# A hybrid encoder on one core: eighteen of the down projection's inner tiles by seven products

## The chip, the core and the metric

One core of one Trainium2 chip. The metric is the device time of one execution in microseconds; the time before is the median of three runs. One of the executions was profiled, and all rows of the trace are from that one.

Engines: PE is TensorE (matmuls, with its weight loads as PEld), DVE is VectorE, ACT is ScalarE, POOL is GpSimd, SP is SyncE, which here only issues DMAs. Each engine does its instructions in the order in which the built program has them.

## The reference

One layer of an encoder over 1024 tokens with 1024 channels, all in float32. The change touches the last part alone, the gated feed-forward and what follows it:

```python
h2 = _rmsnorm(x, ffn_norm_w)
up = h2 @ w_up                                  # 1024 x 5632: gate and value, 2816 columns each
gate = _dwconv_centred(gate, dw_w, dw_b)        # three taps along the tokens
x = x + (silu(gate) * val) @ w_down             # 2816 x 1024
return _rmsnorm(x, final_norm_w)
```

Before it come a projection into the mixers, a convolution module, a chunkwise recurrence in two directions, and the output projection.

## The kernel before

Activations lie with channels on the 128 partitions and tokens along the free dimension, in two halves of 512. So the feed-forward's inner width 2816 is 22 inner tiles of 128 channels (`NF` = 22), and the outer width 8 tiles (`ND` = 8).

Every float32 product is made of three matmuls in a reduced format. An operand is cast to its high part on ACT (`A.copy`, profile L122) and the rest, source minus high part, is made on DVE (L119); together this is `split`. `mm3` (L144 to L146) then adds high x high, high x low and low x high into one PSUM bank. A weight column of `nk` tiles is split at once, in one page of `nk` x 128 columns.

The up projection takes two output tiles as one job, the gate's and the value's of one inner tile j (`ffn_job(j)`, by way of `pair_job`). With the inner sum cut in two (`nk` = 4 tiles each), the outputs in two tiles and the tokens in two halves, this is a 2 x 2 by 2 x 2 block product, and it is made with seven products instead of eight, numbered 1, 2, 6, 7, 5, 4, 3 in the order in which PE does them. Products 1, 6, 5 and 3 go into one bank (`row`, tag mm), each on top of the one before, products 7 and 4 into a second (`col`, tag sc), product 2 into a third (tag tr). After each product the bank is copied or added out before the next one that adds into it; ACT's copies into `su` are L270, the additions on DVE are `evac`, L1278 to L1285.

The weight sides of the seven products are sums of the four weight blocks, and the DMA queues make them. `rows` (tag wr, two buffers) and `col` (tag sw, one buffer) are loaded by SP; POOL then issues DMAs that add into a page on the way (L242): sw <- src1, then wr <- sw into one half of `rows`, then wr <- wr into the other half. `rows` is split twice: as loaded for products 1 and 2, and after both adds for products 6 and 3. `col` is split for products 7 and 5, and a fourth page, w4, for product 4. Weight pages with the splits: four of tag wp, three of tag wq.

`run_jobs` runs a list of such jobs. A job's `run` yields after every two inner tiles (a piece), and the next job's `prep` is called four pieces into the job; `Stream.fill(n)` advances by n pieces. PE's order is the order of the code. For the other engines a scheduler sets the order of the built program, so a cast that stands late in the code can run early.

The feed-forward's gating (in `evac`, L1284 to L1304) runs when the last product of a job has come out: scale by the norm (rstd2), then for each half ACT's first tap (L1289), two taps on DVE (L1293), SiLU on ACT (L1301), two multiplications on DVE (L1302, L1303), and the store of the half to `d_g` in DRAM (L1304).

In its first job the feed-forward waits for the sums of squares: `rstd_over_partitions` (L416 spreads them, L417 copies the result), in the code after seven pieces of job 0. The operands for products 4 and 3 (`hy`) are loaded and split after that (`late_parts`, `late_load`, with an adding DMA, L1334).

The down projection takes inner tiles in groups of 4, 4, 5, 5 and 4. `load_g` brings the tiles of a group from `d_g` and splits them; `std_job` multiplies for each of 8 output tiles and both halves, and `add_evac` (L1369) adds to the result `xr` in SBUF. Its count of matmuls is 22 x 8 x 2 x 3 = 1056. In the last group the residual is added, the tile is turned to tokens on the partitions (`turn_out`, L1410), the sums of squares are taken, and `finish` scales and stores.

Of the kernel before, what the change touches and what calls it, by code (L numbers as in the profile page):

```python
# [10 lines left out]
F32 = mybir.dt.float32  # L11
# [17 lines left out]
BASE_STEPS = 2  # L29
H = 512  # L30
# [15 lines left out]
def tile_hybrid_encoder(  # L46
# [71 lines left out]
    def split_lo(eng, lo, src, hi):  # L118
        eng.tensor_tensor(lo, src, hi.bitcast(F32), op=ALU.subtract)  # L119

    def split(hi, lo, src, eng):
        A.copy(hi, src)  # L122
        split_lo(eng, lo, src, hi)
        return hi, lo
# [22 lines left out]

    def run_jobs(jobs, lead=0, prime=0):  # L150


# [3 lines left out]
        def prepare(n):  # L156
            while jobs and len(ready) < n:
                prep, run = jobs.popleft()
                ready.append((run, prep()))

# [3 lines left out]
        while ready:  # L164
            run, w = ready.popleft()
            pieces = run(w)
            for _ in itertools.islice(pieces, lead):
                yield
            prepare(1)
            yield from pieces  # L170
            prepare(1)
# [53 lines left out]
    def pair_job(src0, src1, nk, acts, wpool, pool, evac, su=4, first=False):  # L225
# [7 lines left out]
        def prep():  # L233
            def both(src, alt):
                hi, lo = split(w_page(2 * nk, alt), w_page(2 * nk, alt), src, V)
                return [(hi[:, :nk], lo[:, :nk]), (hi[:, nk:], lo[:, nk:])]
# [7 lines left out]
            w = {}  # L244
# [6 lines left out]
            add(col, raw_w(src1, 2 * nk) if first else src1)  # L251
            w[1], w[2] = both(rows, None)
            add(rows[:, :nk], col[:, nk:])
            w[7], w[5] = both(col, pool)
            add(rows[:, nk:], rows[:, :nk])
            w[6], w[3] = both(rows, None)
            one = w_page(2 * nk, pool)
            w[4] = split(one[:, :nk], one[:, nk:], a22, V)
            return w

        def run(w):
# [6 lines left out]
            def copy(acc):  # L268
                t = page(pool, "su", su)
                A.copy(t, acc)  # L270
                return t

            row, b2, col = bank("mm"), bank("tr"), bank("sc")
            yield from product(1, row)
            p1 = copy(row)
            yield from product(2, b2)
            evac(0, 0, b2, p1, ALU.add)
            yield from product(6, row, False)
            u2 = copy(row)
            yield from product(7, col)  # L280
            p7 = copy(col)
            yield from product(5, row, False)
            evac(1, 1, p7, row, ALU.subtract)
            yield from product(4, col, False)
            evac(1, 0, col, u2, ALU.subtract)
            yield from product(3, row, False)
            evac(0, 1, row)
# [109 lines left out]
    d_g = scratch("d_g", NF, 2)  # L397

# [836 lines left out]
    h2_pages[7] = [[page(fw, "h7", 2 * NK2, F32R) for _ in range(2)] for _ in range(NK2)]  # L1235
# [27 lines left out]

    fu = tc.alloc_tile_pool(name="fu", bufs=1, reuse_waits="tile")

# [4 lines left out]

    def ffn_job(j):
        g = gp[j % 2]
        val = [None, None]

        def evac(e, half, x0, x1=None, op=None):
            if e == 1:
                val[half] = page(fu, "ft", 4)
# [6 lines left out]
            V.tensor_tensor(g[:, 1 : 1 + H], g[:, 1 : 1 + H], rstd2[0], op=ALU.mult)  # L1284
            V.tensor_tensor(gh, x0, rstd2[1], op=ALU.mult)  # L1285
            for hf in range(2):
                o = hf * H
                c = tmp()
                A.activation(  # L1289
                    c, g[:, o : o + H], AF.Identity, scale=vec("fdw", j), bias=vec("fdb", j)  # L1290
                )
                for k in (1, 2):
                    V.scalar_tensor_tensor(  # L1293
                        c,
                        g[:, o + k : o + k + H],
                        vec("fdw", k * NF + j),
                        c,
                        op0=ALU.mult,
                        op1=ALU.add,
                    )  # L1300
                A.activation(c, c, AF.Silu)  # L1301
                V.tensor_tensor(c, c, rstd2[hf], op=ALU.mult)  # L1302
                V.tensor_tensor(val[hf], val[hf], c, op=ALU.mult)  # L1303
                nc.sync.dma_start(d_g[j][hf], val[hf])  # L1304
# [7 lines left out]
            fu,  # L1312
            evac,
        )

    s_ffn = Stream(run_jobs([ffn_job(j) for j in range(NF)], 4))
# [4 lines left out]
    s_ffn.fill(5)  # L1321
    rstd2 = [next(st) for st in stats]

    def late_parts(i, src):
        h2[i].append(split(page(fu, "hy", 16, F32R), page(fu, "hy", 16, F32R), src, V))

    def late_load(src):
        t = page(fu, "ft", 4)
        nc.sync.dma_start(t, src)
        return t  # L1330

    for k in range(NK2):
        b21 = late_load(d_t6[k])
        G.dma_start(b21, d_h2[k + NK2][0], accum_op=ALU.add)  # L1334
        late_parts(4, b21)
    for k in range(NK2):
        late_parts(3, late_load(d_h2[k + NK2][1]))
    s_ffn.drain()
    fu.release()
    fw.release()  # L1340
# [3 lines left out]

    n_g = itertools.cycle([0] * 32 + [1] * 16)

    def g_page():
        return hx() if next(n_g) == 0 else page(fd, "gx", 16, F32R)

    groups = [4, 4, 5, 5, 4]  # L1350
    gs, jobs = [], []

# [140 lines left out]
```

## Time and profile before

| | us |
|---|---|
| median of three runs | 1862.43 (1860.35 to 1862.73) |
| the profiled execution | 1861.67 |
| its span in the trace | 1859.9 |

| stage, us from the span's start | what |
|---|---|
| up to 1150 | all before the feed-forward |
| 1150 to 1593 | the up projection, 22 jobs |
| 1593 to 1793 | down projection, four groups (18 inner tiles) |
| from 1793 | last group (4 inner tiles), final norm, output |

How to read the rows: the page gives busy time, share of the span and the number of instructions of each engine. A row of the stages gives the stretch, its length, busy time and count for each engine, the granted TensorE clock (1.00 is full), the mean busy share of the 16 DMA engines, and GB/s. A row of the waits gives who waited for which line, us in total, how often, and the longest. A row of the timeline gives start, duration, engine, line, operation and tiles, and in brackets how long the engine was idle before it and what ended that. A row of the chain gives start, duration and what. Successive matmuls overlap: their starts lie closer together than their durations.

### The profile page before, as it was taken

How to read it: one execution, taken by the hardware profiler on the slowest of the kernel's cores; microseconds unless marked ns; L12 is line 12 of the kernel's file. 1: busy time of each engine (PE TensorE's matmuls, PEld its weight loads, DVE VectorE, ACT ScalarE, POOL GpSimd, SP SyncE). 2: the span in 40 equal slices, each digit the busy share in tenths (PEclk: the TensorE clock that was granted, in tenths of full speed). 3: DMA queues.
4: the chain of work that ended last, by engine and by line, in shares of the span. 5: the costliest groups of instructions: out<-in, count | busy, mean ns of one | idle time of the engine just before them, and what ended most of it. 6: DMA issues, size and time to landing. Idle time of an engine off the chain costs nothing.

```text
span 1859.9 us, 23747 instructions
## 1 busy us (share of the span) xinstructions
PE 1778.8 (96%) x8574; PEld 1475.4 (79%) x8574; DVE 1275.2 (69%) x1878; ACT 793.9 (43%) x1482; POOL 172.9 (9%) x189
## 2 busy tenths in 40 slices
PE   8989999999999999999989999899999999999996
PEld 6877877887778888888878787677888888788885
DVE  4599999645479999999835565566666767534445
ACT  6443333334555556555442144443343434522124
POOL 1201111111000000000000001211111111000000
PEclk9999999999999999999999999999999999999998
DMA  7657878874753333332238566876676765733135
GB/s 271 215 146 181 180 175 197 198 173 135 222 170 95 109 114 114 110 105 93 73 120 231 182 210 197 177 163 137 149 155 150 151 155 124 218 95 95 56 87 170
DMA packets 324620, 283.51 MB, mean 152 GB/s; under 512 B 14862, under 2 KB 247062, under 8 KB 324502
## 3 DMA queue, kind: packets, MB, share of 16 engines
q1 hardware_dynamic: 273462, 241.10, 41.5%
q0 software_dynamic: 51040, 40.90, 15.2%
q8 instruction: 67, 1.10, 0.2%
q14 instruction: 51, 0.42, 0.1%
HBM read 189.14 MB, written 72.88 MB: 141 GB/s over the span
## 4 chain that ended last, share of the span: by engine, by line
PE 56%; DVE 20%; DMA 13%; ACT 5%; issue 4%; POOL 1%; SPq 0%; DVEq 0%; ACTq 0%; POOLq 0%
PE mm L144 14%; PE mm L145 14%; PE mm L146 13%; DMA tm<-d_a 3%; PE sc L144 3%; PE sc L146 3%; PE sc L145 3%; DVE wp L119 2%; DVE acc L756 2%; DMA wr<-wr 2%; DVE kG L841 2%; DVE DE L841 2%; DVE qF L841 1%; DMA sw<-in_w_in_dram 1%; DMA wr<-sw 1%
## 5 line engine op out<-in xcount | busy, mean ns | idle before, releaser
L144 PE MATMUL mm<-hx,wp 128*128 128x512 f32 x1176 | 477.4, 406 | 19.4 <-DVE ev L541 7.8
L146 PE MATMUL mm<-hx,wp 128*128 128x512 f32 x1176 | 462.5, 393 | 2.9 <-DVE wp L119 2.9
L145 PE MATMUL mm<-hx,wp 128*128 128x512 f32 x1176 | 462.4, 393 | 1.7 <-DVE hx L476 1.7
L122 ACT CAST wp<-wr 128x1024 fp32r<-128x1024 f32 (+2 forms) x193 | 176.6, 915 | 330.2 <-PE mm L145 191.7
L119 DVE TENSOR_TENSOR wp<-wr,wp 128x1024 fp32r<-128x1024 f32 (+2 forms) x193 | 203.5, 1055 | 111.6 <-ACT wp L122 102.0
L144 PEld LDWEIGHTS mm<-hx,wp 128*128 128x128 f32 x1176 | 223.1, 190 | 66.9 <-DVE ev L541 10.3
L146 PEld LDWEIGHTS mm<-hx,wp 128*128 128x128 f32 x1176 | 222.7, 189 | 53.1 <-DVE wp L119 4.6
L145 PEld LDWEIGHTS mm<-hx,wp 128*128 128x128 f32 x1176 | 223.2, 190 | 43.6 <-DVE hx L476 2.0
L756 DVE SCALAR_TENSOR_TENSOR acc<-gl,v_b,acc 128x1024 f32<-128x1024 f32 x120 | 149.4, 1280 | 0.4
L1369 DVE TENSOR_TENSOR xr<-mm,xr 128x512 f32<-128x512 f32 x48 | 33.2, 691 | 80.6 <-PE mm L146 80.6
L949 PE MATMUL sc<-qF,A 128*128 128x128 f32 x512 | 69.2, 279 | 14.0 <-DVE qF L841 13.2
L949 PEld LDWEIGHTS sc<-qF,A 128*128 128x128 f32 x512 | 64.6, 193 | 20.9 <-issue 16.8
L242 POOL DMA_DIRECT2D wr<-sw x38 | 33.7, 887 | 439.8 <-DVE wp L119 176.0
L122 ACT CAST wq<-sw 128x1024 fp32r<-128x1024 f32 x39 | 41.0, 1051 | 75.0 <-PE mm L145 61.0
L946 ACT COPY A<-kG 128x512 f32<-128x512 f32 x64 | 39.6, 618 | 73.5 <-DVE kG L841 51.0
L1293 DVE SCALAR_TENSOR_TENSOR tm<-gp,v_a,tm 128x512 f32<-128x512 f32 x88 | 65.8, 748 | 2.5 <-ACT tm L1289 1.7
L144 PE MATMUL mm<-hy,wp 128*128 128x512 f32 x156 | 61.2, 393 | 1.9 <-ACT su L270 1.9
L144 PE MATMUL tr<-hx,wp 128*128 128x512 f32 x156 | 61.3, 393 | 0.0
L145 PE MATMUL mm<-hy,wp 128*128 128x512 f32 x156 | 61.2, 392 | 0.0
L144 PE MATMUL sc<-hy,wq 128*128 128x512 f32 x156 | 61.1, 392 | 0.0
L146 PE MATMUL sc<-hy,wq 128*128 128x512 f32 x156 | 61.0, 391 | 0.0
L145 PE MATMUL sc<-hy,wq 128*128 128x512 f32 x156 | 60.8, 390 | 0.0
(322 smaller groups left out, 3573.1 us busy)
## 6 DMA issues: line engine op xcount, KB each, us to landing
wr<-in_w_in_dram SPq DMA_DIRECT2D x53, 512.0 KB, 4.9
sw<-in_ffn_w_up_dram SPq DMA_DIRECT2D x44, 256.0 KB, 4.7
sw<-in_ffn_w_up_dram POOLq DMA_DIRECT2D x22, 512.0 KB, 8.7
wr<-in_ffn_w_up_dram SPq DMA_DIRECT2D x22, 512.0 KB, 7.0
d_g<-ft SPq DMA_DIRECT2D x44, 256.0 KB, 3.8
ev<-d_g SPq DMA_DIRECT2D x44, 256.0 KB, 3.4
wr<-sw POOLq DMA_DIRECT2D x38, 256.0 KB, 3.2
wr<-wr POOLq DMA_DIRECT2D x38, 256.0 KB, 4.8
```

Source lines behind the costliest of these rows:

```text
L119: eng.tensor_tensor(lo, src, hi.bitcast(F32), op=ALU.subtract)
L122: A.copy(hi, src)
L144: T.matmul(acc, whi[:, k, :], ahi, start=first, stop=False, skip_group_check=again)
L145: T.matmul(acc, whi[:, k, :], alo, start=False, stop=False, skip_group_check=again)
L146: T.matmul(acc, wlo[:, k, :], ahi, start=False, stop=last, skip_group_check=again)
L242: G.dma_start(o, a, accum_op=ALU.add)
L756: V.scalar_tensor_tensor(acc, g[:, k : k + S], tap(k), acc, op0=ALU.mult, op1=ALU.add)
L841: V.tensor_tensor(o, a, b, op=op)
L946: A.copy(A_t.rearrange("p (b x e) -> p b x e", x=2, e=h), pairs(kG, h))
L949: T.matmul(b[:, c * P : (c + 1) * P].rearrange("p (b x e) -> p b x e", x=2, e=h), A_t[:, c * P : (c + 1) * P], view(qF, c * P, [[2 * h, P ...
L1293: V.scalar_tensor_tensor(c, g[:, o + k : o + k + H], vec("fdw", k * NF + j), c, op0=ALU.mult, op1=ALU.add,)
L1369: V.tensor_tensor(xr[i][half], acc, xr[i][half], op=ALU.add)
```

## The change

It has three parts.

1. The first 18 inner tiles of the down projection, as three groups of six, go by seven products too: `down_seven(n, m)` takes two output tiles and six inner tiles (`nk` = 3) as one job of `pair_job`, 12 jobs in all, in the same stream as the feed-forward's jobs. The seven activation sides are three of the four blocks themselves and four sums of them. `down_operands` makes the sums on DVE in the feed-forward and SP stores them in `d_t`: jobs at places 3, 4 and 5 of each six load their partner's tiles back (`mate`, from `d_g[j - 3]`), so that it is called nine times, each time at the end of `gated(1)`, which runs in the job after. The seven products are added straight to `xr` (`taps`). The last four inner tiles go by `std_job` as before, half by half.
2. Casts and gating are spread over pieces. `pair_job`'s `prep` becomes a generator of steps (`Weights`): loads at once, the split for products 1 and 2 three pieces later, that for 7 and 5 four later, for 6 and 3 three later, for 4 three later. `gated(hf)` is put off by 3 and 5 pieces with `later`. The operands of the down projection come in by a list of events: a load four pieces ahead of its split. The parts for products 4 and 3 of the feed-forward's operands are put off in the same way.
3. `pin` (`tc.keep_in_program_order`) keeps the scheduler from moving these casts, their subtractions and the two activations of the gating (all but the last job's) from their place in the code.

```diff
+    pin = tc.keep_in_program_order
+
+    def split(hi, lo, src, eng, late=False):
+        parts = A.copy(hi, src), eng.tensor_tensor(lo, src, hi.bitcast(F32), op=ALU.subtract)
+        if late:
+            for i in parts:
+                pin(i)
         return hi, lo
...
+    class Weights:
+        def __init__(self, steps):
+            self.parts = {}
+            self.steps, self.wait = steps(self.parts), 0
+            self.tick()
+
+        def tick(self):
+            self.wait -= 1
+            if self.wait <= 0:
+                self.wait = next(self.steps, 1 << 30)
+
+        def __getitem__(self, i):
+            while i not in self.parts:
+                self.wait = 0
+                self.tick()
+            return self.parts[i]
...
             for _ in itertools.islice(pieces, lead):
+                tick()
                 yield
             prepare(1)
...
+            yield 3
             w[1], w[2] = both(rows, None)
             add(rows[:, :nk], col[:, nk:])
+            add(rows[:, nk:], rows[:, :nk])
+            yield 4
             w[7], w[5] = both(col, pool)
-            add(rows[:, nk:], rows[:, :nk])
+            yield 3
             w[6], w[3] = both(rows, None)
+            yield 3
             one = w_page(2 * nk, pool)
-            w[4] = split(one[:, :nk], one[:, nk:], a22, V)
-            return w
+            w[4] = split(one[:, :nk], one[:, nk:], a22, V, late)
...
+    def down_operands(k, b11, b12, b21, b22):
+
+        t7, t6 = ft(), ft()
+        V.tensor_tensor(t7, b12, b22, op=ALU.subtract)
+        V.tensor_tensor(t6, t7, b11, op=ALU.subtract)
+        V.tensor_tensor(b12, b11, b12, op=ALU.subtract)
+        V.tensor_tensor(b11, b21, t6, op=ALU.add)
+        for i, t in ((7, t7), (6, t6), (5, b12), (4, b11)):
+            nc.sync.dma_start(d_t[i - 4][k], t)
...
+        def gated(hf):
...
+            V.tensor_tensor(val[hf], val[hf], c, op=ALU.mult)
+            nc.sync.dma_start(d_g[j][hf], val[hf])
+            if hf == 1 and mate:
+                down_operands(3 * group + place - 3, *mate, *val)
...
             for hf in range(2):
...
+                later(3 + 2 * hf, lambda hf=hf: gated(hf))
+            if group < NSEVEN and place >= 3:
+                for hf in range(2):
+                    mate.append(ft())
+                    nc.sync.dma_start(mate[hf], d_g[j - 3][hf])
...
+    def down_seven(n, m):
+        def taps(i, acc):
...
+            t = xr[2 * m + e][half]
+            if n > 0:
+                V.tensor_tensor(t, t, acc, op=op)
+            elif i in (1, 6, 7, 3):
+                A.copy(t, acc)
...
+        return pair_job(
+            cols(2 * m), cols(2 * m + 1), 3, lambda i: ops[n][i], fw, fv, None, late=True, taps=taps
+        )
...
+    def come_in(at, dst, src):
...
+        events.append((at - 4, 0, load_it))
+        events.append((at, 1, parts))
+
+    for n in range(NSEVEN):
+        loads = [operand(n, i, k) for i in PRODUCTS for k in range(3)]
+        if n == 0:
+            at = [PAIR * (NF - 1) + 3 + x + x // 9 for x in range(21)]
+        else:
+            at = [PAIR * (NF + 4 * n - 4) + 16 + 4 * x for x in range(5)]
+            at += [PAIR * (NF + 4 * n - 1) + 3 + int(1.2 * x) for x in range(16)]
...
-    groups = [4, 4, 5, 5, 4]
...
+    for half in range(2):
+        st = Stream(run_jobs(down_jobs(f0, NF - f0, (half,), final_evac)))
```

`PAIR` is 14, the pieces of a job; `NSEVEN` is 3, the groups of six. In the last feed-forward job product 3 is done ahead of product 4, in a bank of its own (`apart`). The output is stored in halves of its width, from pages of 512 columns.

308 lines of the change are left out of this document (191 added, 117 removed).

## The prediction

> **What bounds the kernel now.** I read the page first, then the busy time by stage, then PE's waits from the feed-forward on, then one steady feed-forward job on all engines.
>
> ```profile
> span 1859.9 us, 23747 instructions
> PE 1778.8 (96%) x8574; PEld 1475.4 (79%) x8574; DVE 1275.2 (69%) x1878; ACT 793.9 (43%) x1482; POOL 172.9 (9%) x189
> ```
> ```profile
> core 0: us, PE busy (x) PEld busy (x) DVE busy (x) ACT busy (x) POOL busy (x), PEclk, DMA share, GB/s
> 1314.00:1545.00 231.00, 231.00 (x1007) 188.93 (x1006) 154.18 (x204) 95.04 (x132) 39.75 (x37) 1.00 0.71 152
> 1700.00:1798.00 98.00, 98.00 (x434) 81.22 (x433) 35.93 (x52) 13.09 (x19) 0.00 (x0) 1.00 0.18 51
> ```
> ```profile
> PE sc L416 <- ACT rs L417: 6.1, 1, 6.1
> PE mm L144 <- ACT su L270: 4.9, 4, 1.6
> PE mm L144 <- ACT xr L1363: 3.2, 1, 3.2
> ```
>
> PE is the bound: no idle time in steady feed-forward and down projection. One matmul costs 231/1007 = 0.229 us in the feed-forward and 98/434 = 0.226 us in the down projection. What PE waits for is small: 6.1 us where the feed-forward starts, 4.9 us for copies of early products, 3.2 us at the seam to the down projection. The DMA engines are 71% busy in the feed-forward and 18% in the down projection: what makes weights for seven products is dear in transfers.
>
> The steady feed-forward job, rows of the timeline by engine:
>
> ```profile
> 1399.57 0.69 DVE L1285 TENSOR_TENSOR gp<-mm,rs 128x512 f32<-128x512 f32 x1 [1.35 <-PE mm L146]
> ...
> 1402.83 1.23 DVE L119 TENSOR_TENSOR wp<-wr,wp 128x1024 fp32r<-128x1024 f32 x1 [1.79 <-ACT wp L122]
> 1404.07 0.69 DVE L1302 TENSOR_TENSOR tm<-tm,rs 128x512 f32<-128x512 f32 x1
> ...
> 1409.20 1.22 DVE L119 TENSOR_TENSOR wp<-wr,wp 128x1024 fp32r<-128x1024 f32 x1
> ...
> 1418.85 0.69 DVE L1285 TENSOR_TENSOR gp<-mm,rs 128x512 f32<-128x512 f32 x1 [1.36 <-PE mm L146]
> ```
> ```profile
> 1401.75 1.05 ACT L122 CAST wp<-wr 128x1024 fp32r<-128x1024 f32 x1 [4.26 <-DMA wr<-wr]
> ...
> 1406.72 0.63 ACT L1301 ACTIVATE tm<-tm 128x512 f32<-128x512 f32 x1 [2.22 <-DVE tm L1293]
> ...
> 1420.16 1.05 ACT L122 CAST wp<-wr 128x1024 fp32r<-128x1024 f32 x1 [3.40 <-DMA wr<-wr]
> ```
> ```profile
> 1396.42 0.84 POOL L242 DMA_DIRECT2D wr<-wr  x1 [2.66 <-DMA wr<-sw]
> 1402.63 1.57 POOL L242 DMA_DIRECT2D sw<-in_ffn_w_up_dram  x1 [5.37 <-DMA sw<-in_ffn_w_up_dram]
> 1411.79 0.87 POOL L242 DMA_DIRECT2D wr<-sw  x1 [7.58 <-DMA d_g<-ft]
> 1415.30 0.85 POOL L242 DMA_DIRECT2D wr<-wr  x1 [2.64 <-DMA wr<-sw]
> 1421.43 1.56 POOL L242 DMA_DIRECT2D sw<-in_ffn_w_up_dram  x1 [5.28 <-DMA sw<-in_ffn_w_up_dram]
> ```
> ```profile
> 1415.48 0.38 SPq L247 DMA_DIRECT2D sw<-in_ffn_w_up_dram  x1
> ```
>
> A job lasts 1418.85 - 1399.57 = 19.28 us (84 matmuls at 0.229). Call the subtraction at 1402.83 s63 (low parts of products 6 and 3, this job) and the one at 1409.20 s12 (products 1 and 2, next job). They are tied in a ring: s63 -> later work in DVE's order -> s12 -> POOL adds into the same rows (wr<-sw, then wr<-wr) -> cast and s63 of the next job, without which PE cannot do product 6, the third of seven. That POOL waits for s12 a row of an earlier job shows:
>
> ```profile
> 1140.74 1.23 DVE L119 TENSOR_TENSOR wp<-wr,wp 128x1024 fp32r<-128x1024 f32 x1 [0.17 <-ACT wp L122]
> ```
> ```profile
> 1142.26 0.88 POOL L242 DMA_DIRECT2D wr<-sw  x1 [146.77 <-DVE wp L119]
> ```
>
> The ring now: s63 end to s12 end 1410.42 - 1404.06 = 6.4; start of POOL 1142.26 - 1141.97 = 0.3; wr<-sw 1415.30 - 1411.79 = 3.5; wr<-wr 1420.16 - 1415.30 = 4.9; cast to s63 end 1404.06 - 1401.75 = 2.3. Sum 17.4 us, 1.9 below the job, so PE never sees it.
>
> **The change, part by part.**
>
> *Matmuls.* The built program has 108 fewer: 864 become 756. Before 864 x 0.226 = 195.1 us; after, at the feed-forward's pitch (weights come the same way), 756 x 0.229 = 173.4: -21.7 us, if nothing else waits.
>
> *Plain feed-forward jobs.* gated() is now called 3 and 5 pieces into the next job, and the casts are held in program order. In the built order DVE now runs, between s63 and s12: the split of operand 4, four L1293, two L1302, two L1303, two evacuations; all of the gating work, part of which ran ahead of s63 before. That is 11 operations; eight took 1409.20 - 1404.07 = 5.13 us, 0.64 each, so 7.0. The second SiLU (0.63, ACT) has nothing on DVE beside it: +0.75 with two hand-overs. Directly dependent neighbours and the first SiLU's rest: +0.4, an estimate. s12 itself 1.2. So 9.4 in place of 6.4, and the ring is 9.4 + 0.3 + 3.5 + 4.9 + 2.3 = 20.4 us: longer than 19.3. PE waits 1.1 us at product 6 of each such job. There are 11: +12 us.
>
> *Jobs with down_operands* (9, places 4, 5, 0 of each six). Four more subtractions or additions and one evacuation stand ahead of s12: 5 x 0.64 = 3.2. Ring 23.6, +4.3 a job. In the third of each three the built order puts s63 behind three other operations, so only 13 remain between: 8.3 + 0.75 + 1.2 = 10.3, ring 21.3, +2.0. Sum 6 x 4.3 + 3 x 2.0 = +32. Their six extra transfers (2 loads, 4 stores of 256 KB) are SP's, ahead of the next sw load; that load's own chain has slack while the ring waits.
>
> Of the 4.9 us of L270 waits, in four pauses, one (1.6) stands at the start; the other 3.3 are replaced. Feed-forward: 12 + 32 - 3.3 = +41. Bounds: if both adds take 3.5 us, plain jobs lose nothing and the nine lose 2.9, 2.9, 0.6: +16 after the same deduction. If wr<-wr takes 1401.75 - 1396.42 = 5.3, and the extra transfers (1.57 MB beside 2.9 MB a job, on engines 71% busy) add 3 us in the nine: 11 x 1.5 + 6 x 7.7 + 3 x 5.4 - 3.3 = +75. I take the steady row.
>
> A rule of the Trainium skill speaks for the lower bound. "DMA: Bandwidth & Descriptors", section "Anatomy of one DMA", puts a transfer issued by GpSimd at about 2.0 us fixed plus bytes/436e3: 2.6 us for 256 KB, one add like the other. By it the ring would be 9.4 + 0.3 + 5.2 + 2.3 = 17.2 and plain jobs would lose nothing. The trace disagrees: 3.5 and 4.9.
>
> *The feed-forward's start.*
>
> ```profile
> 1150.33 0.39 PE L146 MATMUL mm<-mg,wp 128*128 128x512 f32 x1
> 1150.56 0.39 PE L144 MATMUL mm<-hx,wp 128*128 128x512 f32 x1
> ...
> 1173.63 0.45 PE L146 MATMUL sc<-h,wq 128*128 128x512 f32 x1
> ```
> ```profile
> 1158.09 0.69 DVE L119 TENSOR_TENSOR hx<-tm,hx 128x512 fp32r<-128x512 f32 x1 [1.18 <-ACT hx L122]
> ```
> ```profile
> 1161.48 2.68 POOL L1334 DMA_DIRECT2D ft<-d_h  x3 [3.19 <-DMA ft<-d_t]
> ```
> ```profile
> 1603.70 0.71 PE mm L144
> 1604.41 0.43 PE mm L145
> ...
> 1607.38 0.24 PE mm L146
> ```
>
> Before, job 0's split ran early and PE went on at 1150.56 without a pause. Now it is held in order behind the last operand splits (the last ran at 1158.09). With less between them I put its cast's end at 1157.2 and s12 at 1158.5: PE pauses 6.6 us. After the 3.2 us pause at the seam matmuls took 0.43 us, for 8 of them: +1.6. Products 1 and 2 then end about 1164. wr<-sw lands at 1158.8 + 3.5; the three L1334 stand on POOL before wr<-wr, until 1165; wr<-wr 4.9, cast and s63 2.3: 1172.4, a second pause. The remaining 18 matmuls before the spread (4.1 + 1.6) and the spread itself (2 us) end at 1180; before, that point was passed at 1173. +7 us, though the 6.1 us wait for rs goes (rs now stands ahead of the hy casts). Bounds -6 (only that wait goes) to +10.
>
> *Down jobs.* PE needs 63 x 0.229 = 14.4 us. The chain through sw: product 5 ends at 10.3, cast and subtraction of 768 columns until 12.2; sw load, POOL's add of src1, wr<-sw, wr<-wr, cast and s63; product 6 of the job after next. In the feed-forward these take 1421.43 - 1415.48 = 5.95, 1411.79 - 1402.63 = 9.2, 3.5, 4.9, 2.3. At three quarters of the size, between three quarters of the time and all of it; the engines will be busier (3.15 MB in 14.4 us is 219 GB/s, against 152 at 71%), so nearer to all. Ends: 12.2 + 18.0 + 1.8 = 32.0 = 2T + 4.5, T = 13.8, so PE's 14.4; or 12.2 + 23.6 + 1.8, T = 16.5. I take 15.6: 12 x 15.6 = 187. By the skill's rule above the smaller adds would save 0.15 us each, the upper end. At both group seams 16 operands come in within some 20 pieces, and DVE has 16 splits, 7 additions and 4 weight splits per job in its order: 4 us each, an estimate from those counts. At the first seam ACT's copy of product 1 stands behind gated() of the last job and four operand casts (some 9.8 us into a job that needs it at 4.1): 6, and 1.6 of slow clock: 7 with rounding. Sum 202; before 195.1 + 3.2 + 1.6 = 200: +2 (-20 with PE alone and no seam cost; +25 with T = 17.5). So the whole gain in matmuls is spent.
>
> *Rest.* Before the last output-projection tiles the order is unchanged. The last four inner tiles are computed as before; twice the output stores of half the size at the end: +1.
>
> *Sum* on the profiled span: 1859.9 + 41 + 7 + 2 + 1 = 1910.9; the median of the runs, 1862.43, is 2.5 above that span: **1913 us**.
>
> **Rivals.**
>
> Faster: the two adds run at 3.5 us and are no longer crossed by sw loads. Place: product 6 of each feed-forward job; it decides from 7.3 us for both on (9.4 + 0.3 + 7.3 + 2.3 = 19.3). For it: wr<-sw's own 3.5; against: 4.9 and 5.3 beside it. Feed-forward +16, start 0, down jobs at PE's pace with half the seam cost -20: 1858; it falls to 1840 if down_operands is also absorbed. Chance 0.14. The skill's fixed-cost rule is this case.
>
> Transfers bound the down jobs: T = 17.5 and the seams with it, +23 on the forecast, 1936. For it: 219 GB/s against 152 at 71%; against: plain loads cost less, 51 GB/s at 18%. Chance 0.17.
>
> The pauses halve the clock and PE is on the path: nine pauses of some 4 us, 8 matmuls x 0.2 = 1.6 each, 14 us: 1927. Against: while the ring runs PE has that time to spare, so I hold it hidden. Chance 0.10. "TensorE: Matmul & The Clock Gate", Part 1, of the Trainium skill has the clock halve after an idle window of about 3.4 us; the seam's rows agree (3.2 us).
>
> The ring binds only in the nine jobs: feed-forward +28, start +7, down -10: 1888 or less, with the odd case that all cancels. Chance 0.09. That the change does less than it says is excluded by the built program's 108 fewer matmuls.
>
> **How the numbers follow.** Forecast 0.50 (own range 1890 to 1930). Two kernels of this length can be told apart from about 0.2%, 3.7 us. Faster 0.14 (the first rival), same 0.04 (out of the fourth), slower 0.82. The range 1858 to 1946 leaves out the fast half of the first rival and the worst of the second.
>
> **What would show it.** In the changed profile: PE idle at product 6 (L147 matmuls into mm) put down to wp's subtraction, near 1 us in plain jobs and 4 in the nine; POOL wr<-sw starting 0.3 us after s12; job length 20.4 and 23.6; down jobs near 15.6; a pause before the first feed-forward product. Wrong if feed-forward jobs stay at 19.3, or down jobs at 14.4.

## The result and the profile after

With the change the kernel takes 1962.55 us (median of four runs, 1955.0 to 1963.9) against 1861.39 us in the runs beside it: 1.054 times as long, 95% interval 1.051 to 1.058. The forecast was 1913 us with a range of 1858 to 1946: the sign was right, half of the loss was missed, and the time lies above the range.

The page of the changed kernel, its span and the busy times:

```profile
span 1959.5 us, 24020 instructions
PE 1796.3 (92%) x8466; PEld 1470.7 (75%) x8466; DVE 1340.7 (68%) x1982; ACT 822.8 (42%) x1530; POOL 212.0 (11%) x225
```

PE has 108 matmuls fewer and is busy longer: 18 us more in a span 99.6 us longer. PE's waits (who waited for which line, us in total, times, longest) tell where:

```profile
PE mm L147 <- ACT wp L123: 35.6, 9, 6.2
PE mm L147 <- ACT su L336: 24.2, 15, 2.8
PE mm L147 <- ACT xr L1451: 19.2, 4, 12.7
...
PE mm L147 <- DVE xr L1449: 12.4, 7, 3.4
```

Nearly all of it is at product 6 (L147 into mm), the third of seven. The exceptions are 5.7 us ahead of the first product, 4.0 us of the second row that lie ahead of the feed-forward, and 2.2 us at products 5 and 3 of the down projection. The first two rows are mostly the feed-forward, where ACT's cast of the rows for products 6 and 3, or the copy of product 1 queued behind it, comes late. The last two rows are the down projection, 12.7 us of them at its first seam.

The busy time by stage, the feed-forward's steady part and the twelve down jobs:

```profile
1314.00:1545.00 231.00, 209.49 (x848) 164.45 (x847) 138.75 (x188) 77.64 (x110) 33.52 (x31) 0.94 0.65 153
1690.00:1893.00 203.00, 178.85 (x735) 142.90 (x734) 118.52 (x176) 69.38 (x117) 33.90 (x32) 0.95 0.71 173
```

In the stretch that held 1007 matmuls before there are 848, at a mean granted clock of 0.94 in place of 1.00, and the DMA engines are less busy (0.65 against 0.71): bandwidth is not what is short, something waits. The last evacuation of a feed-forward job (L1285 before, L1400 after; duration, then first and last start) gives the length of the 20 jobs from job 0's to job 20's (before, job 20 ends at 1573.1; the row's last start is job 21's):

```profile
L1285 DVE TENSOR_TENSOR gp<-mm,rs x22: 685/694/694, 1183.4 to 1593.3; 128x512 f32<-128x512 f32 x22
```
```profile
L1400 DVE TENSOR_TENSOR gp<-mm,rs x21: 679/692/694, 1194.0 to 1651.4; 128x512 f32<-128x512 f32 x21
```

The 99.6 us of the two spans divide so: +67.7 in these 20 jobs (457.4 against 389.7), +9.5 ahead of them (job 0 ends 42.5 us after the output projection, not 33.1), +1.1 in job 21, +20.1 from the first down matmul to the end (287.9 against 267.8), +1.2 in the stages before, which are not edited.

The ring of the prediction, in a plain job (first rows) and in a job with down_operands (later rows), from the timeline of each engine (start, duration, engine, line, operation, in brackets the idle time before it and what ended it):

```profile
1357.48 1.22 DVE L123 TENSOR_TENSOR wp<-wr,wp 128x1024 fp32r<-128x1024 f32 x1 [4.14 <-ACT wp L123]
...
1366.84 1.22 DVE L123 TENSOR_TENSOR wp<-wr,wp 128x1024 fp32r<-128x1024 f32 x1
...
1378.55 1.23 DVE L123 TENSOR_TENSOR wp<-wr,wp 128x1024 fp32r<-128x1024 f32 x1 [5.53 <-ACT wp L123]
...
1451.96 1.23 DVE L123 TENSOR_TENSOR wp<-wr,wp 128x1024 fp32r<-128x1024 f32 x1 [3.99 <-ACT wp L123]
...
1459.56 0.69 DVE L1381 TENSOR_TENSOR tm<-tm,rs 128x512 f32<-128x512 f32 x1 [2.65 <-ACT tm L1380]
...
1464.18 1.22 DVE L123 TENSOR_TENSOR wp<-wr,wp 128x1024 fp32r<-128x1024 f32 x1
...
1476.19 1.22 DVE L123 TENSOR_TENSOR wp<-wr,wp 128x1024 fp32r<-128x1024 f32 x1 [7.07 <-ACT wp L123]
```
```profile
1368.59 0.89 POOL L299 DMA_DIRECT2D wr<-sw  x1 [9.81 <-DVE wp L123]
1372.09 0.86 POOL L299 DMA_DIRECT2D wr<-wr  x1 [2.60 <-DMA wr<-sw]
...
1465.93 0.89 POOL L299 DMA_DIRECT2D wr<-sw  x1 [12.93 <-DVE wp L123]
1469.46 0.86 POOL L299 DMA_DIRECT2D wr<-wr  x1 [2.64 <-DMA wr<-sw]
```
```profile
1377.48 1.04 ACT L123 CAST wp<-wr 128x1024 fp32r<-128x1024 f32 x1 [9.78 <-DMA wr<-wr]
...
1450.88 1.04 ACT L123 CAST wp<-wr 128x1024 fp32r<-128x1024 f32 x1 [4.48 <-DMA wr<-wr]
...
1457.47 0.59 ACT L336 COPY su<-mm 128x512 f32<-128x512 f32 x1 [4.31 <-PE mm L149]
1457.95 1.05 ACT L123 CAST wp<-wr 128x1024 fp32r<-128x1024 f32 x1
1458.90 0.63 ACT L1380 ACTIVATE tm<-tm 128x512 f32<-128x512 f32 x1
```

Plain: start of s63 at 1357.48, s12 at 1366.84 (9.4 later), wr<-sw 1.75 after that (1.2 of it s12 itself), 3.5, wr<-wr and its wait 5.4, cast 1.1: the next s63 comes 21.1 us after the first. The later job: 12.2, 1.75, 3.5, 5.65, 1.1: 24.2. In it DVE waits 2.65 us for the second SiLU, and the SiLU stands behind ACT's copy of product 6, for which ACT waits 4.31 us: PE itself is in the ring there.

### The profile page after: what moved, and what is told of

Read it like the earlier page. It is cut to its first block, busy times and chain, and to the rows that moved or that the text cites. A ratio compares the mean times of both kernels' runs of the same rounds, so it can differ in the third digit from the quotient of the medians.

```text
span 1959.5 us, 24020 instructions
## 1 busy us (share of the span) xinstructions
PE 1796.3 (92%) x8466; PEld 1470.7 (75%) x8466; DVE 1340.7 (68%) x1982; ACT 822.8 (42%) x1530; POOL 212.0 (11%) x225
## 3 DMA queue, kind: packets, MB, share of 16 engines
q1 hardware_dynamic: 291286, 264.70, 42.7%
## 4 chain that ended last, share of the span: by engine, by line
PE 33%; DVE 26%; DMA 25%; ACT 7%; issue 7%; POOL 1%; SPq 0%; DVEq 0%; ACTq 0%; POOLq 0%
DMA wr<-wr 9%; PE mm L147 8%; PE mm L149 8%; PE mm L148 8%; DMA wr<-sw 7%; DVE wp L123 4%; DMA tm<-d_a 2%; DVE kG L912 2%; ACT wp L123 2%; DVE acc L827 2%; PE sc L147 2%; DVE qF L912 2%; DVE DE L912 2%; PE sc L148 2%; PE sc L149 2%
## 5 line engine op out<-in xcount | busy, mean ns | idle before, releaser
L147 PE MATMUL mm<-hx,wp 128*128 128x512 f32 x1020 | 430.4, 422 | 92.6 <-ACT wp L123 35.6
L149 PE MATMUL mm<-hx,wp 128*128 128x512 f32 x1020 | 415.2, 407 | 3.2 <-DVE wp L123 2.4
L148 PE MATMUL mm<-hx,wp 128*128 128x512 f32 x1020 | 411.7, 404 | 1.8 <-DVE hx L547 1.8
L123 ACT CAST wp<-wr 128x1024 fp32r<-128x1024 f32 (+2 forms) x185 | 175.1, 946 | 383.2 <-DMA wr<-wr 252.5
L147 PEld LDWEIGHTS mm<-hx,wp 128*128 128x128 f32 x1020 | 199.9, 196 | 143.3 <-ACT wp L123 44.4
L149 PEld LDWEIGHTS mm<-hx,wp 128*128 128x128 f32 x1020 | 199.3, 195 | 60.6 <-DVE wp L123 16.5
L148 PEld LDWEIGHTS mm<-hx,wp 128*128 128x128 f32 x1020 | 200.5, 197 | 39.3 <-DVE hx L547 2.1
L299 POOL DMA_DIRECT2D wr<-sw x50 | 44.7, 894 | 475.7 <-DVE wp L123 246.7
L123 ACT CAST wq<-sw 128x1024 fp32r<-128x1024 f32 (+1 forms) x51 | 51.1, 1003 | 94.9 <-PE mm L148 63.0
L336 ACT COPY su<-mm 128x512 f32<-128x512 f32 x78 | 45.3, 581 | 102.8 <-PE mm L149 101.6
L1020 PEld LDWEIGHTS sc<-qF,A 128*128 128x128 f32 x512 | 65.1, 194 | 20.8 <-issue 16.7
L147 PE MATMUL tr<-hx,wp 128*128 128x512 f32 x172 | 67.4, 392 | 0.0
L148 PE MATMUL tr<-hx,wp 128*128 128x512 f32 x172 | 66.9, 389 | 0.0
L149 PE MATMUL tr<-hx,wp 128*128 128x512 f32 x172 | 66.9, 389 | 0.0
L147 PE MATMUL mm<-hy,wp 128*128 128x512 f32 x152 | 60.4, 398 | 4.1 <-ACT su L336 4.1
L147 PE MATMUL sc<-hy,wq 128*128 128x512 f32 x156 | 61.2, 392 | 0.0
L149 PE MATMUL sc<-hy,wq 128*128 128x512 f32 x156 | 61.0, 391 | 0.0
```

The costliest lines, as they stand in the source:

```text
L123: parts = A.copy(hi, src), eng.tensor_tensor(lo, src, hi.bitcast(F32), op=ALU.subtract)
L147: T.matmul(acc, whi[:, k, :], ahi, start=first, stop=False, skip_group_check=again)
L148: T.matmul(acc, whi[:, k, :], alo, start=False, stop=False, skip_group_check=again)
L149: T.matmul(acc, wlo[:, k, :], ahi, start=False, stop=last, skip_group_check=again)
L299: G.dma_start(o, a, accum_op=ALU.add)
L336: A.copy(kept[i], acc)
```

## The experiments

Each run was profiled, and what follows is read by stage, since the unedited stages alone end the output projection anywhere from 1146.9 to 1157.2 us in these runs. Columns: from the end of the output projection to the end of job 0; 20 feed-forward jobs; the twelve seven-product down jobs; the time (one run unless an interval is given below).

| run | job 0 | 20 jobs | down | time |
|---|---|---|---|---|
| before | 33.1 | 389.7 | | 1861 |
| after | 42.5 | 457.4 | 221.8 | 1962.6 |
| e1_gate_one_piece | 42.8 | 408.7 | 221.3 | 1913.2 |
| e2_gate_after | 43.1 | 394.9 | 214.3 | 1892.4 |
| e3_no_operands | 43.3 | 425.6 | 220.4 | 1935.4 |
| e4_first_free | 35.4 | 458.3 | 219.4 | 1958.3 |
| e5_row_adds_dve_ffn | 42.5 | 383.2 | 215.8 | 1879.7 |
| e6_row_adds_dve_down | 43.0 | 457.7 | 191.2 | 1936.1 |
| e7_not_held | 33.9 | 409.1 | 218.3 | 1902.1 |
| e8_three_edits | 33.1 | 402.7 | 195.2 | 1868.5 |
| e9_operations_only | 43.1 | 447.8 | 218.6 | 1945.0 |
| e10_adds_dve_all | 36.9 | 384.3 | 192.5 | 1846.4 |
| e11_first_copy_dve | 35.7 | 383.8 | 192.4 | 1849.0 |
| e12_adds_dve_plain_down | 35.5 | 383.5 | | 1858.7 |
| e13_first_add_dve | 42.7 | 460.1 | 205.5 | 1944.5 |
| e14_second_add_dve | 43.6 | 460.3 | 212.3 | 1955.1 |

**The order on DVE.** e1 changes one number:

```diff
-                later(3 + 2 * hf, lambda hf=hf: gated(hf))
+                later(3 + 1 * hf, lambda hf=hf: gated(hf))
```

> One number of the change is edited: the second half's gating starts 4 pieces into the next job, not 5. In the built order DVE then has s12 ahead of the second half's last two products and of all four operations of down_operands. Theory (ring): from the start of s63 to the start of s12 it takes 7.7 us in every job, against 9.35 in plain jobs and 12.2 to 14.7 in the nine; with 1.75 to the first row add, 3.5 and 5.4 for the adds and 1.1 for the cast the ring is 19.4 us, and with slower adds 20.3 in the nine. The 20 steady feed-forward jobs fall from 457 us to about 396, the whole from 1961 to about 1900. Rival (transfers: the six extra transfers of the nine jobs make them long, whatever the order): the nine stay above 23 us and only the plain jobs gain, about 1939. Rival (PE's clock after pauses is the cost): as the pauses go, so does it; it can't be told apart here from the ring.

The 20 jobs lost 48.7 us of the 67.7. From s63 to s12 it took 7.24 us in nearly every job, the nine included; fourteen jobs took 19.1 to 20.2. Six, all behind down_operands, still took 21.4 to 23.6 us. There a wait that the theory had not named took over: POOL's first row add.

```profile
1259.87 1.58 POOL L299 DMA_DIRECT2D sw<-in_ffn_w_up_dram  x1 [6.33 <-DMA sw<-in_ffn_w_up_dram]
1269.86 0.89 POOL L299 DMA_DIRECT2D wr<-sw  x1 [8.41 <-DVE ft L1353]
```

s12 had ended at 1267.60, but the add began at 1269.86, 10.0 us after POOL's add into sw was issued. The releaser named, an operation of down_operands (L1353), is not an input of the add. What the add needs besides s12 is the add into sw, and the trace has that landing at 1268.70, after s12. In the other five the row add starts 0.5 to 0.6 us after that landing (in the next job 1292.93 after 1292.31, with s12 done at 1290.38), and in the job after those two it starts at 1313.66, before that job's L1353 has run (1314.73). So what it waits for is the add into sw, which takes 8.8 us in the rows shown (why 1.2 us more pass there stays open), and the rival with the six transfers has a part too.

e2 moves the gating behind s12:

```diff
-                later(3 + 2 * hf, lambda hf=hf: gated(hf))
+                later(9 + 2 * hf, lambda hf=hf: gated(hf))
```

> The gating of a job starts 9 and 11 pieces into the next one, behind s12. Theory (ring): between s63 and s12 only PE's product 6, its copy and the cast are left, 4.5 us; the ring is 4.5 + 1.75 + 3.5 + 5.4 + 1.1 = 16.2 us, shorter than PE's 19.3, so all jobs run at 19.3 to 19.6 and the feed-forward's 20 steady jobs take 388 us in place of 457; the whole about 1891. The four operations of down_operands now stand ahead of s63: at most 1 us in each of the nine jobs. Rival (transfers): the nine jobs stay 3 us or more longer than the plain ones, about 1920.

394.9 us where 388 was expected, and the whole within 2 us of the expected. The nine are at 19.3 to 20.0 us but one (21.9). In eight of them PE pauses for 0.3 to 0.5 us, for a subtraction that now stands behind down_operands.

**What of it are the operands.** e3 takes down_operands, its stores and loads out; e9 leaves its four operations and takes out the loads and stores.

```diff
-            if group < NSEVEN and place >= 3:
+            if False:
```

> Left out: the sums and differences of down_operands, their four stores and the two loads of each of the nine jobs; the down projection reads other tiles in their place (the same loads and products, other data). Theory (ring): all feed-forward jobs are plain ones of 21.1 us; the 20 steady jobs fall from 457 to about 422 us, the whole to about 1926. Rival (the transfers alone make the ring long, also in the plain jobs): plain jobs fall below 20.5 us and the whole below 1915. Rival (DVE's part is nothing, the nine are long from PE's clock): below 10 us of gain.

425.6 us: all jobs are plain, 21.3 us each. That is the ring's 21.1 and no gain below it, so the plain jobs' 2 us have nothing to do with the extra transfers. (The time itself, 1935, holds 5.7 us by which the stages before ended later.)

```diff
-        V.tensor_tensor(t7, b12, b22, op=ALU.subtract)
...
-        for i, t in ((7, t7), (6, t6), (5, b12), (4, b11)):
-            nc.sync.dma_start(d_t[i - 4][k], t)
+        V.tensor_tensor(t7, b21, b22, op=ALU.subtract)
+        V.tensor_tensor(t6, t7, b21, op=ALU.subtract)
+        V.tensor_tensor(t5, b21, b22, op=ALU.subtract)
+        V.tensor_tensor(t4, b21, t6, op=ALU.add)
```

> Left out: the two loads and four stores of 256 KB in each of the nine jobs; the four DVE operations of down_operands stay, on tiles of the job itself, and the down projection reads other tiles (the same loads and products, other data). Theory (ring: what counts of the nine is DVE's and ACT's order, the transfers only through the length of the two adds): the nine keep 12.6 to 13.5 us between the starts of s63 and s12 and lose some 0.5 us of the adds; the 20 steady jobs take 445 to 454 us in place of 457. Rival (the six transfers make the nine long): the 20 jobs fall to 430 us or less, as in the run without down_operands at all (425.6).

447.8 us, inside the range of the ring: of the 32 us that down_operands costs, some 22 are the place of its four operations, and 10 the transfers. With the transfers gone the nine have 12.0 us from s63 to s12, a little below the 12.6 to 13.5 expected.

**The two transfers themselves.** e5 leaves every order as it is and takes POOL's two row adds out of the ring.

```diff
-            add(rows[:, :nk], col[:, nk:])
-            add(rows[:, nk:], rows[:, :nk])
             yield 4
+            for o, a in ((rows[:, :nk], col[:, nk:]), (rows[:, nk:], rows[:, :nk])):
+                pin(V.tensor_tensor(o, o, a, op=ALU.add))
```

(for j > 0 in the feed-forward; elsewhere the old lines.)

> The order of the gating stays as the change has it; in feed-forward jobs 1 to 21 the two adds into the rows (wr<-sw and wr<-wr, 128x512 each) are done by DVE, 11 pieces into the job before, ahead of the split for products 7 and 5, not by POOL's accumulating DMAs. Theory (ring, whose long legs are these two transfers): 1.75 + 3.5 + 5.4 us of the ring become some 3 us on DVE; plain rings 15 us, the nine 17 to 18, both below PE's 19.2. The 20 steady jobs fall from 457 to about 390 us, the whole from 1961 to about 1893, although DVE does 1.2 us more in every job. Rival (DVE's order alone is the cost): jobs stay above 21 us. Rival (the other transfers of the nine jobs): these stay above 21 us, about 1915.

```profile
1314.00:1545.00 231.00, 231.00 (x1014) 190.09 (x1014) 186.15 (x254) 96.65 (x133) 19.10 (x13) 1.00 0.65 165
```

The feed-forward's steady part has no pause at all: PE busy for 231 of 231 us, clock 1.00, in spite of 186 us of DVE work where there were 139. 383.2 us is 6.5 less than before the change and 7 less than expected. Pauses of 3.3 us that stood in these 20 jobs before (PE busy for 386.4 of 389.7 us) went too; the rest is a closer pitch, 1014 matmuls in 231 us where there were 1007, and why they came closer is not shown. With e1 and e2 this shows the ring from both sides: take time out of DVE's leg or out of the transfers, and PE's pauses go.

**The start and the holding.**

```diff
-            late=True,
+            late=j > 0,
```

> Job 0 of the feed-forward alone has its casts as before the change, not spread and not held in order. Theory: the two pauses of 6.1 and 6.6 us at the feed-forward's start go, a wait of about 6 us for the statistics comes back, and job 0 ends 8 to 11 us earlier: the whole about 1951. Rival (the operand splits, held in order, are what PE waits for): the gain is under 4 us.

(6.1 and 6.6 us are counted from the start of the matmul ahead; PE was idle for 5.7 and 6.2.) Job 0 ended 7.1 us earlier, a little short of 8, and PE's two pauses for the cast went. A new one of 4.4 us came, for the held operand splits (hy): the rival's part. The whole fell by 4 us only, since the stages before ended 5.0 us later.

```diff
-    pin = tc.keep_in_program_order
+    pin = lambda i: i
```

> All casts and gating steps stay where the change issues them, but nothing is held in program order: the planner places them. In the built order DVE has both halves' gating spread around s63 and the operations of down_operands behind s12: eight operations between s63 and s12, 6.9 us with s63. Theory (ring): 6.9 + 1.75 + 3.5 + 5.4 + 1.1 = 18.7 us in plain jobs, hidden; up to 20 in the nine; the 20 steady jobs about 392 us; job 0 no longer held gives another 7 us; the down jobs, bound by transfers, stay at 222. The whole about 1890. Rival (the delay of the casts, not the holding, is the cost): above 1940.

409.1 us for the 20 jobs where 392 was expected, 1902 where 1890: seven tenths of the loss in the feed-forward go away with the holding of the steps in order, and the rest stays with where the change issues them.

**The down jobs.** e6 makes the same edit as e5 in the twelve down jobs alone.

> The same in the twelve seven-product jobs of the down projection alone; the feed-forward stays as the change has it. Theory (latency of a chain of transfers through sw and the rows, T = 17.5 us a job): the chain loses two transfers of 3.3 and 5.8 us and gains 1.2 us on DVE: 12.2 + 5.5 + 8.4 + 1.2 + 0.9 = 28.2 = 2T + 4.5, T = 11.9, so PE's 14.4 is the bound; with the seam to the feed-forward as it is, the twelve jobs take 196 us in place of 222, the whole about 1935. Rival (the DMA engines are full: bandwidth, not latency): T stays above 16.5 us, the whole above 1948.

191.2 us. From product 7 of one job to that of the next it takes 15.2 us on average, where it took 17.5, and five of the eleven take PE's 14.3 us. The DMA engines were not full (0.71 in the changed kernel, 0.63 here): it was latency, not bandwidth. A pause of 8 us at the first seam stays. Which chain it was e13 and e14 ask: only the first row add, or only the second, goes to DVE.

```diff
+                yield 4
+                pin(V.tensor_tensor(rows[:, :nk], rows[:, :nk], col[:, nk:], op=ALU.add))
+                add(rows[:, nk:], rows[:, :nk])
```

> The change as it is, but in the twelve down jobs the first row add (the one that reads sw) is done by DVE; the second stays POOL's DMA. Theory A (ring of one job through sw: load 5.5, POOL's add 8.3, wr<-sw 3.3 until sw may be loaded again): the ring loses wr<-sw and gains 0.6, so it ends near 14.5 to 15.5 a job; the twelve jobs take 192 to 200 us in place of 222, the whole about 1936. Theory B (ring through the rows and s12, 17 us): the first add's place in DVE's order comes later than its DMA did, so 15 to 16 us, the whole about 1942. The chain of the prediction (two jobs, released by the cast of products 7 and 5): PE's 14.4. All three fall here; the next run tells them apart.

205.5 us, above the 192 to 200 of theory A; the average is 16.5 us a job, and no theory gave that.

```diff
+                add(rows[:, :nk], col[:, nk:])
+                yield 4
+                pin(V.tensor_tensor(rows[:, nk:], rows[:, nk:], rows[:, :nk], op=ALU.add))
```

> The change as it is, but in the twelve down jobs the second row add (rows into rows) is done by DVE; the first, which reads sw, stays POOL's DMA. Theory A (ring of one job through sw, 5.5 + 8.3 + 3.3 and the hand-overs): untouched, a job stays at 17 us or more; only the wait at the seam shrinks by some 4 us; the twelve jobs take 212 to 220 us, the whole about 1954. Theory B (ring through the rows, of which the second add is 5.8): falls to PE's 14.4, the whole about 1935. The chain of the prediction (12.2 + 5.5 + 8.4 + 3.3 + 0.6 + 0.9 = 2T + 4.5): T = 13.2, so PE's 14.4, the whole about 1935.

212.3 us, as theory A has it and some 15 us above what the other two give; the average is 16.9. What SP waits for in the down jobs (us in total, times, longest), in the changed kernel and in e14, and then the transfers of one round in the changed kernel, on SP and on POOL:

```profile
SPq L303 <- DMA wr<-sw: 27.1, 10, 6.8
```
```profile
SPq L303 <- DMA wr<-sw: 53.8, 10, 10.0
```
```profile
1700.94 0.38 SPq L303 DMA_DIRECT2D sw<-in_ffn_w_down_dram  x1
...
1717.52 0.38 SPq L303 DMA_DIRECT2D sw<-in_ffn_w_down_dram  x1
```
```profile
1701.09 0.86 POOL L299 DMA_DIRECT2D wr<-wr  x1 [4.34 <-DMA wr<-sw]
1706.08 1.46 POOL L299 DMA_DIRECT2D sw<-in_ffn_w_down_dram  x1 [4.14 <-DMA sw<-in_ffn_w_down_dram]
1714.34 0.89 POOL L299 DMA_DIRECT2D wr<-sw  x1 [6.80 <-DMA sw<-in_ffn_w_down_dram]
1717.57 0.86 POOL L299 DMA_DIRECT2D wr<-wr  x1 [2.33 <-DMA wr<-sw]
```

SP's load of sw starts when the first row add, which reads sw, has landed (POOL's second add starts at the same moment). Load 5.1, POOL's add into sw 8.3, wr<-sw 3.2: 16.6 us, and 17.9 on average from 1700.94 to 1861.63 (nine rounds). That is a ring of one job. In six of the nine rounds the load starts within 0.14 us of that landing; in the other three, the one shown among them, the split of sw for products 7 and 5, which reads sw as well, ends after that landing.

In the three edited runs that split is the last to let sw go: the load starts 0.03 us after it in every round, since the edits put it behind a row add in DVE's order. So the second add's move (e14) did not leave the ring untouched; it kept wr<-sw in it and put the split behind. The means of nine rounds, in us, with the job's average (T) beside them:

| run | load | POOL's add into sw, and wait for the first row add | first row add | until the next load | round | T |
|---|---|---|---|---|---|---|
| after | 5.1 | 8.8 | 3.7 | 0.3 | 17.9 | 17.5 |
| e13 | 4.9 | 10.1 | 0.6 | 1.1 | 16.7 | 16.5 |
| e14 | 3.9 | 8.7 | 3.1 | 1.5 | 17.2 | 16.9 |
| e6 | 3.8 | 9.3 | 0.6 | 1.5 | 15.2 | 15.2 |

The round goes with T in all four. e13 gained less than expected because DVE's row add started 10.1 us after POOL's issue on average, up to 3.8 us after the add into sw had landed, and the split followed it. What held the add back on DVE is not shown. In e14 some jobs take 14.3 us, but two at the group seams take 21 to 22 and give it back.

**Together.** e8 is e2, e4 and e6; e10 is e5, e4 and e6.

> Gating behind s12 (as in the run that starts it 9 and 11 pieces in), job 0's casts free, and the row adds of the twelve down jobs on DVE. Theory: the three act in different stages and add up: 1892 - 7 - 26 = 1859 us, that is the time before within 6 us. Rival (the three hide one another, since one stage's late end covers the next one's): above 1875.

> The row adds by DVE in feed-forward jobs 1 to 21 and in the twelve down jobs, and job 0's casts free. Theory: the three stages add up: job 0 ends 33 us after the output projection (42.5 with the change), the 20 steady jobs 383 us (457), the twelve down jobs 193 us (222), the rest as it was: 1846 us, 0.8 per cent below the time before. Rival (one stage's late end covers the next): above 1862.

e8 gave 1868.5, 9 us above the sum, 8 of it in the 20 jobs, which do not repeat e2's to the microsecond: in three jobs PE waited 1.9 to 2.7 us for ACT's copy of product 1, in e2 in one. e10 gave 1846.43 us (1842.66 to 1850.84) against 1863.04 beside it: 0.991 times the time before, interval 0.989 to 0.993. It has the lowest median of all, and was forecast at 1846. That it meets the forecast so closely is luck in part: the profiled execution took 1850.84, and job 0 ended 36.9 us after the output projection where 33 was expected.

> As the last, and at the seam the copy of product 1 in the first group's jobs is made by DVE, not by ACT, where it stood behind the last job's gating. Theory: the 8 us wait for that copy shrinks to some 4, since DVE's order has the same gating and splits ahead of it but no SiLU to wait for: 4 us below the last run. Rival (DVE's order is as full): no gain or a loss of up to 2 us.

```diff
+            elif i == 1:
+                V.tensor_copy(t, acc)
```

No gain: 1848.99 us, 0.993 (0.991 to 0.996). PE's wait at the seam was 9.2 us against 6.6 in e10: DVE's order was as full, as the rival had it.

> The feed-forward as in the run with all three edits, without the operations of down_operands, and the down projection as before the change (864 matmuls, no seven products). Theory: feed-forward as there (383 us for 20 jobs), the down projection and what follows 268 us as before: 1852 to 1856 us. So the seven products of 18 tiles are worth 6 to 10 us where nothing waits for transfers, not the 21.7 us of their matmuls. Rival (the seven-product down projection is a loss even so): below 1846.

(The feed-forward of e10, without down_operands, and the down projection of before in place of the twelve jobs.) 1858.71 us, 0.998 (0.997 to 1.000). So with the row adds on DVE the seven products are worth 12.3 us (1858.71 - 1846.43), more than the 6 to 10 expected and not the 21.7 that their matmuls come to; part of the rest is the pause at the first seam, 6.6 us in e10 and 3.7 in e12.

## Why the prediction was right or wrong

**Sign and place were right, and in the feed-forward the mechanism.** The matmuls do go, and what takes their place there is the ring through s12 and POOL's two adds, at product 6. The plain job's DVE leg was forecast at 9.4 us and is 9.4. Two steps failed: the ring of the nine jobs was priced too short, and the chain of the down jobs was the wrong one. The span came out 48.6 us above the forecast's 1910.9. Of these, 28 lie in the feed-forward, 19 of them in the nine jobs, and 17 from the first down matmul on.

**Plain jobs: two legs too short.** Forecast 20.4, measured 21.1. POOL starts 0.5 us after s12, not 0.3, and wr<-wr with its wait is 5.4, not 4.9. Seven tenths of a microsecond on a job of 20 is little, but of a pause of 1.1 us it is two thirds; with a few longer ones it comes to 21.3 a job, 18 us in 20 jobs (e3: 425.6; the same 20 jobs at 20.4 would be 408). In the changed kernel the eleven plain jobs cost 20 us, where 12 was forecast.

**The nine jobs: PE and the extra transfers were in the ring.** Forecast 23.6, 23.6 and 21.3; one group of three measured 25.0, 26.3 and 24.2. All nine cost 51 us more than jobs of 19.3, where +32 was forecast. Two terms were too small, by some 9 us each over the nine jobs.

The first is DVE's leg. The prediction counted DVE's operations and gave the second SiLU 0.75 us. In the first job of the group that held: the wait was 0.70 and the leg 12.6, as forecast. In the second and third, SiLU stood on ACT behind the copy of product 7 or 6, and that behind PE: the waits were 1.66 and 2.65. In the rows above ACT cast until 1451.92, PE then took until 1457.47 for product 6, 5.5 us for 12 matmuls that take 2.7 at full clock. So the slow clock that the third rival put on the path, and that I held hidden, was on it here. In plain jobs it was hidden, as I said: in e3 jobs with eleven slow matmuls and jobs with three have the same leg from s63 to s12, 9.4 us.

The second is what follows s12. POOL starts 0.5 us after it, once 1.2, not 0.3, and the two adds took 8.6 to 9.9 us, not 8.4. The forecast put the six extra transfers at nothing, except in its upper bound; e9 shows that they count, since without them the 20 jobs are 10 us shorter.

**Feed-forward in sum.** +41 was forecast with bounds of 16 and 75; it is +68.8 with job 21. The bounds held, the middle did not.

**The start.** +7 forecast, +9.5 measured, with two pauses of 6.1 and 6.6 us (from the start of the matmul ahead) where the text had 6.6 and a second one. e4 gives 7.1 of it back.

**The down jobs: the wrong chain.** Here the mechanism failed, and not only a size. The prediction released SP's load of sw by the cast for products 7 and 5 and got T from two jobs: 32.0 = 2T + 4.5. It left out that wr<-sw reads sw too, later in most rounds, so that load, add into sw and wr<-sw make a ring of one job: 17.9 us a round, T 17.5. The rows for it stood in the prediction, 5.95 + 9.2 + 3.5 = 18.6 us a job in the feed-forward, hidden there under 19.3. Between three quarters of that and all of it, and nearer to all, as the prediction had it for its own chain, it would have put PE's 14.4 almost out of reach. The twelve jobs were forecast at 202 us with the seams and took 221.8. T is that of the second rival, but by another way: that rival had the DMA engines fuller, from 219 GB/s, and they were 71% busy at 173. Its time (1936) was short because it kept the feed-forward's +41.

**The first seam.** 7 us forecast, slow clock included. Measured, PE is idle for 12.7, and the nine matmuls of product 6 then take 1.8 us longer than at full clock: ACT's copy of product 1 was held up by gating and operand casts, as said, and these in turn by the cast for product 6, which waited for the row adds:

```profile
1681.46 0.83 ACT L123 CAST wp<-wr 128x768 fp32r<-128x768 f32 x1 [8.72 <-DMA wr<-wr]
...
1687.99 0.57 ACT L1451 COPY xr<-mm 128x512 f32<-128x512 f32 x1
```

**The length of the two adds.** "DMA: Bandwidth & Descriptors", "Anatomy of one DMA", of the Trainium skill gave the faster rival its 2.6 us an add. The page of the profile shows 3.3 and 5.2 us to landing for the two in the mixers' and feed-forward's pair jobs: the measurement decides, and that rival is out.

**The range.** It treated the long feed-forward and the slow down jobs as alternatives. They share a cause, transfers in series that must end within one job, and came together: 1913 + 28 + 17 is within 5 us of the result. Two slips in the sums changed nothing: three quarters of the down chain's four transfers are 17.7 us, not 18.0, and the lower bound of -20 for the down jobs still holds the first seam's 7.

## What to carry to other kernels

Where a tile is filled, read, added to by DMA and read again within one job, write down for each such tile the loop of everything that must end before it may be written again: the longest loop bounds the job, however idle the engines are. Holding steps in order puts whatever stands between two of its links into the loop, so ask what is queued between them on every engine, PE included. A short add on an engine with time to spare can be worth far more than its own time if it takes a transfer's latency out of such a loop: here 1.2 us of DVE work a job took 74 us out of the feed-forward.

## What the runs showed of the hardware

Smaller transfers were not faster in proportion. The page's DMA issues (size of one, median us to landing) for the two row adds, larger in the feed-forward and mixers, smaller in the down jobs:

```profile
wr<-sw POOLq DMA_DIRECT2D x38, 256.0 KB, 3.3
wr<-wr POOLq DMA_DIRECT2D x38, 256.0 KB, 5.2
...
wr<-sw POOLq DMA_DIRECT2D x12, 192.0 KB, 4.0
wr<-wr POOLq DMA_DIRECT2D x12, 192.0 KB, 4.3
```

The first add even took longer. The DMA engines were busier beside the smaller ones (0.71 against 0.65), so how much of this is the size is not shown.

And the slow clock does not follow the length of one pause. In e3 PE was idle for 1.60 us up to 1247.43, and eleven slow matmuls followed; it was idle for 2.70 us up to 1590.84, and three followed (a row of PE for each, then the stretch, with columns as above and the clock behind POOL's):

```profile
1247.43 0.50 PE L147 MATMUL mm<-hx,wp 128*128 128x512 f32 x1 [1.60 <-ACT su L336]
1590.84 0.50 PE L147 MATMUL mm<-hx,wp 128*128 128x512 f32 x1 [2.70 <-ACT su L336]
```
```profile
1245.50:1253.00 7.50, 5.86 (x18) 4.09 (x17) 5.94 (x9) 4.71 (x8) 1.58 (x1) 0.77 0.64 92
1587.80:1595.00 7.20, 4.46 (x19) 3.11 (x18) 4.53 (x7) 4.12 (x7) 1.58 (x1) 1.00 0.56 75
```

The Trainium skill, "TensorE: Matmul & The Clock Gate", Part 1, says that the activity window is free-running and that the number of slow matmuls differs with its phase. These rows agree with that in kind: the cost depends on more than the pause's length. Nor did the slow clock take 3.4 us of idle time here, the figure in the prediction's third rival: 1.60 us came ahead of the eleven.
